# The first 512 features of each squared-ReLU layer computed as plain products, with the sums of activations made behind them

## The chip, the cores and the metric

The program runs on one NeuronCore of a Trainium2 chip. Five engines work side by side, each through its own instructions in its own order: TensorE (PE, with its weight loads shown apart as PEld), VectorE (DVE), ScalarE (ACT), GpSimd (POOL) and SyncE (SP), which here issues the transfers from device memory. An instruction waits on semaphores for what it needs from another engine, and whatever stands behind it on its engine waits too. The metric is the time of one execution on the device in microseconds (us); lower is better.

## The reference

The model is a stack of two layer pairs on 512 tokens of 1024 features: attention, a squared-ReLU layer, a gated recurrent block, a second squared-ReLU layer, and a last norm. The change touches the two squared-ReLU layers and the norm ahead of each:

```
def rmsnorm(x, g):
    y = xf * lax.rsqrt(jnp.mean(xf * xf, axis=-1, keepdims=True) + RMS_EPS)
    return (y * g.astype(jnp.float32)).astype(x.dtype)

def sq_relu_mlp(h, w1, w2):
    z = jax.nn.relu(jnp.einsum('bsd,df->bsf', h, w1))
    return jnp.einsum('bsf,fd->bsd', z * z, w2)
...
h = h + sq_relu_mlp(rmsnorm(h, norm_mlp[layer]), mlp_w1[layer], mlp_w2[layer])
```

Here w1 is 1024 x 4096 and w2 is 4096 x 1024, all in float32.

## The kernel before

Activations are held transposed: eight tiles hT[k] of 128 features by 512 tokens. To keep float32 accuracy on TensorE every operand is split into a high part (a cast to fp32r, by ACT) and a low part (the rest, by DVE), and `mm3` (L175) makes three matmuls of each product: high x high, high x low, low x high. So each weight unit (128 x 1024 numbers, 512 KB) costs a transfer (L104 or L110), an ACT cast into `wh` (L118) and a DVE subtraction into `wl` (L119). `plan` lists all units in the order in which TensorE wants them; `fetch` makes one, `want(n)` keeps `ahead` units made beyond the n that it hands out. Units live in the pool `wsp` (5 buffers); inside a squared-ReLU layer four more come from the pool `wx`, taken in turns of nine (L92). A unit's buffer is free when TensorE has read the unit that had it before. Raw weights go through three buffers `wr`.

A squared-ReLU layer (`mlp`, L530) handles the 4096 hidden features in eight groups g of 512. `up(g)` makes the group's first product by a seven-product scheme on 2 x 2 blocks (256 tokens or features to a block, Strassen's in Winograd's form): seven products named 1 to 7 of 24 matmuls of 128 x 256 each, in place of eight. It needs sums of weight blocks (units of kinds s1 to s4, five DVE additions of 128 x 1024 a group, L115 and L116) and sums of activation blocks t1 to t4. The latter are made once a layer: t1 where the norm's gain is applied (`split` with `blocks`, L203 to L207), and t2 to t4 by `sums_of` (L538), into tH and tL. `down(g, m)` makes the second product in plain form, 12 matmuls of 128 x 512 for each of eight tiles m of the output, and adds to hT[m]. Downs of group g-1 stand between the products of group g.

The norm's factor per token is taken late: the products run on activations that have only the gain, the squares are summed over features (`square`, L209, then `sums`, whose four little matmuls fill ss, then a square root on ACT and a reciprocal on DVE), and `rstd` (four more little matmuls, an ACT copy) spreads the factor `r` over partitions. It is used in `relu2` (L577). The work ahead of layer 0 is the last part of the attention's output projection (matmuls "wo", L333), ahead of layer 1 the recurrent block's ("ro", L812 and L814); after each tile of it `feed(m)` applies the gain.

The order on each engine is set by a scheduler ahead of time from the order of the calls and its own estimates; at run time it is fixed.

Of the kernel before, what the change touches and what calls it, by code (L numbers as in the profile page):

```python
# [15 lines left out]
P = 128  # L16
# [24 lines left out]
def trunk(ctx: ExitStack, tc: tile.TileContext, xT, cols, win, wqkv, wo, rwin, rga, rgx, rwo, w1, w2, out):  # L41
# [44 lines left out]
    def fetch():  # L86
# [65 lines left out]
    def add_mlp(layer):  # L152
        starts.append(len(plan))
        for g in range(9):
            if g < 8:
                rows, cs = (slice(0, T), slice(T, D)), (slice(g * T, g * T + U), slice(g * T + U, (g + 1) * T))
                srcs = [w1[layer][rows[k], cs[c]] for k, c in ((0, 0), (0, 1), (1, 1), (1, 0))]
                up_ = [(kind, 4, srcs) for kind in ("11", "s1", "12", "22", "s2", "s4", "s3")]
            else:
                up_ = []  # L160
            dn = [("plain", 4, [w2[layer][(g - 1) * T : g * T, u * U : (u + 1) * U]]) for u in range(4)] if g else []
            if up_ and dn:
                plan.extend(up_[0:2] + dn[0:1] + up_[2:3] + dn[1:2] + up_[3:5] + dn[2:3] + up_[5:7] + dn[3:4])
            else:
                plan.extend(up_ + dn)

# [5 lines left out]
    add_mlp(1)  # L172
    state["stop"] = starts[0]

# [16 lines left out]
    class Norm:  # L191
        def __init__(self, name, gain, c0=0, n=T, blocks=False):
            self.name, self.gain, self.acc, self.last, self.c, self.n = name, gain, None, None, slice(c0, c0 + n), n
            self.blocks, self.psum = blocks, mmp if blocks else atp

        def split(self, k):
            g = cst[:, self.gain + k : self.gain + k + 1]
            if not self.blocks or k >= KT // 2:
                S.activation(hnH[k], hT[k], AF.Copy, scale=g)
                V.scalar_tensor_tensor(hnL[k], hT[k], g, f(hnH[k]), ALU.mult, ALU.subtract)  # L200
# [21 lines left out]
        def feed(self, k):  # L222
            if k == 0:
                tc.keep_in_program_order(S.activation(spare, epsb, AF.Sqrt))
            self.split(k)
            if not self.blocks:
                self.square(k)


        def sums(self):  # L230
            nt = self.n // P
            ss = self.psum(f"{self.name}ss")
            parts = [self.acc] if self.last is None else [self.acc, self.last]
# [9 lines left out]
        def rstd(self):  # L243
            nt = self.n // P
            row = self.psum(f"{self.name}row")
            for t in range(nt):
# [8 lines left out]
    n0 = Norm("n0", C_MIX0)  # L255
    nm1 = Norm("nm1", C_MLP0, blocks=True)
    with ExitStack() as actx:
# [272 lines left out]
    def mlp(ly, norm, nxt, halves):  # L530
        with ExitStack() as mctx:
            pool = lambda name, bufs: mctx.enter_context(tc.tile_pool(name=f"{name}{ly}", bufs=bufs))
            sr, wx, tp, cp, zp = pool("sr", 1), pool("wx", 4), pool("t", 1), pool("c", 1), pool("z", 2)
            state.update(raw=sr, more=wx, units=0, ahead=7, stop=starts[ly + 1] if ly + 1 < len(starts) else None)
            prefetch(4)
            z, r, tH, tL = {}, [], [], []

            def sums_of(k):  # L538
                g, g2 = (cst[:, norm.gain + j : norm.gain + j + 1] for j in (k, k + 4))
                a = wk.tile([P, T], F32, name=f"ha{ly}{k}", tag="nsq", bufs=2)  # L540
                S.activation(a, hT[k], AF.Copy, scale=g)
                H = tp.tile([P, 3, U], F32R, name=f"tH{ly}{k}", tag=f"tH{k}")
                L = tp.tile([P, 3, U], F32R, name=f"tL{ly}{k}", tag=f"tL{k}")
                raw = cp.tile([P, 2, T], F32, name=f"ht{ly}{k}", tag="cB" if k % 2 else "cA")
                raw = raw.rearrange("p i (j c) -> p (i j) c", j=2)

                V.scalar_tensor_tensor(raw[:, 2], hT[k + 4][:, HI], g2, a[:, HI], ALU.mult, ALU.subtract)
                V.tensor_add(raw[:, 1], raw[:, 2], a[:, LO])
                V.scalar_tensor_tensor(raw[:, 0], hT[k + 4][:, LO], g2, raw[:, 1], ALU.mult, ALU.subtract)
                S.activation(H[:, 0:2], raw[:, 0:2], AF.Copy, scale=-1.0)  # L550
                V.scalar_tensor_tensor(L[:, 0:2], raw[:, 0:2], -1.0, f(H[:, 0:2]), ALU.mult, ALU.subtract)  # L551
                S.copy(H[:, 2], raw[:, 2])
                V.tensor_sub(L[:, 2], raw[:, 2], f(H[:, 2]))
# [10 lines left out]
            B11, t1, B21, B22 = own(0, LO), own(0, HI), own(4, LO), own(4, HI)  # L564
            t4, t2, t3 = (sum_(n) for n in range(3))

# [8 lines left out]

            def relu2(g, n, c, op, rr_):
                V.scalar_tensor_tensor(c, c, 0.0, rr_[:, None, :].to_broadcast([P, 2, T]), op, ALU.mult)  # L577
                S.activation(c, c, AF.Square)
# [4 lines left out]
                for i in range(2):  # L583
                    z[g, 2 * n + i] = (zH[:, i], zL[:, i])

            def up(g):

                acc = {}

                def one(n, xs):  # L590
                    acc[n] = (mmp if g == 0 and n in "54" else atp)(f"p{n}{ly}{g}")
                    product(acc[n], xs)
                    acc[n] = pair(acc[n])
# [19 lines left out]
                V.tensor_add(cA[:, :, HI], acc["3"], cA[:, :, HI])  # L613
                relu2(g, 0, cA, ALU.max, r[0])
                yield
# [3 lines left out]
                V.tensor_add(cB[:, :, HI], acc["5"], w)  # L619
                relu2(g, 1, cB, ALU.min, r[0])  # L620
                yield
# [59 lines left out]

    nm2 = Norm("nm2", C_MLP1, blocks=True)
    with ExitStack() as rctx:
# [172 lines left out]
```

## Time and profile before

| | us |
|---|---|
| median of three executions | 1104.23 (1103.11 to 1105.21) |
| the profiled execution | 1108.84 |
| its span, first to last instruction | 1107.1 |
| PE busy | 1080.5 (98%) |
| DVE busy | 875.9 (79%) |
| ACT busy | 538.5 (49%) |
| granted TensorE clock, mean | 0.989 |

A row of a timeline reads: start, duration, engine, line, operation, out<-in by the program's names, shape, count, and in brackets how long the engine stood idle before it and what ended that. A row of a view by windows gives for a stretch of time the busy microseconds of each engine with the number of instructions, the clock that TensorE was granted (1.00 is full), the share of the transfer engines' time and the rate. Matmul rows overlap, since they are pipelined: the step from one start to the next is what a matmul takes from TensorE, not its duration.

### The profile page before, as it was taken

How to read it: one execution, taken by the hardware profiler on the slowest of the kernel's cores; microseconds unless marked ns; L12 is line 12 of the kernel's file. 1: busy time of each engine (PE TensorE's matmuls, PEld its weight loads, DVE VectorE, ACT ScalarE, POOL GpSimd, SP SyncE). 2: the span in 40 equal slices, each digit the busy share in tenths (PEclk: the TensorE clock that was granted, in tenths of full speed). 3: DMA queues.
4: the chain of work that ended last, by engine and by line, in shares of the span. 5: the costliest groups of instructions: out<-in, count | busy, mean ns of one | idle time of the engine just before them, and what ended most of it. 6: DMA issues, size and time to landing. Idle time of an engine off the chain costs nothing.

```text
span 1107.1 us, 16096 instructions
## 1 busy us (share of the span) xinstructions
PE 1080.5 (98%) x6424; PEld 962.2 (87%) x6424; DVE 875.9 (79%) x1316; ACT 538.5 (49%) x794; POOL 11.0 (1%) x28
## 2 busy tenths in 40 slices
PE   9999999997999999999999999899999999999996
PEld 7889988887899899999988888789899999899996
DVE  7998888788886886777767689988897786777655
ACT  7766665465443443433435497456453343343321
POOL 1000000000000000000000000000000000000000
PEclk9999999998999999999999999999999999999998
DMA  8532441332334324313241122432433333323102
GB/s 266 136 101 72 115 118 55 109 100 77 100 92 152 96 62 138 105 58 115 59 151 58 58 76 77 123 124 82 129 107 103 116 95 94 106 82 99 57 1 77
DMA packets 113786, 109.10 MB, mean 99 GB/s; under 512 B 4016, under 2 KB 110640, under 8 KB 113712
## 3 DMA queue, kind: packets, MB, share of 16 engines
q1 hardware_dynamic: 113568, 108.02, 32.2%
q8 instruction: 50, 0.82, 0.3%
q14 instruction: 24, 0.20, 0.1%
q10 hardware_dynamic: 144, 0.07, 0.0%
HBM read 101.78 MB, written 2.10 MB: 94 GB/s over the span
## 4 chain that ended last, share of the span: by engine, by line
PE 82%; DVE 11%; DMA 3%; ACT 2%; issue 2%; SPq 0%; DVEq 0%; ACTq 0%
PE d L176 10%; PE d L177 10%; PE d L178 10%; PE p L176 9%; PE p L178 9%; PE p L177 9%; DVE wl L119 2%; PE x L384 1%; PE xb L176 1%; PE xb L178 1%; PE xb L177 1%; ACT wh L118 1%; DMA wr<-in_wqkv 1%; PE v L176 1%; PE oa L400 1%
## 5 line engine op out<-in xcount | busy, mean ns | idle before, releaser
L118 ACT CAST wh<-b 128x1024 fp32r<-128x1024 f32 x112 | 115.9, 1049 | 203.1 <-DVE b L116 76.8
L177 PE MATMUL d<-zL,wh 128*128 128x512 f32 (+1 forms) x544 | 205.9, 379 | 0.0
L176 PE MATMUL d<-zH,wh 128*128 128x512 f32 (+1 forms) x544 | 205.3, 380 | 0.0
L178 PE MATMUL d<-zH,wl 128*128 128x512 f32 (+1 forms) x544 | 204.7, 377 | 0.0
L119 DVE TENSOR_TENSOR wl<-b,wh 128x1024 fp32r<-128x1024 f32 x112 | 135.6, 1223 | 48.0 <-ACT wh L118 48.0
L118 ACT CAST wh<-wr 128x1024 fp32r<-128x1024 f32 (+1 forms) x121 | 125.7, 1041 | 94.7 <-PE p L177 45.6
L119 DVE TENSOR_TENSOR wl<-wr,wh 128x1024 fp32r<-128x1024 f32 (+1 forms) x121 | 146.8, 1213 | 21.7 <-ACT wh L118 21.5
L176 PE MATMUL p<-hnH,wh 128*128 128x256 f32 x512 | 147.2, 288 | 4.8 <-ACT wh L118 3.9
L178 PE MATMUL p<-hnH,wl 128*128 128x256 f32 x512 | 147.0, 287 | 2.1 <-DVE wl L119 2.1
L177 PE MATMUL p<-hnL,wh 128*128 128x256 f32 x512 | 147.3, 288 | 0.0
L178 PEld LDWEIGHTS d<-zH,wl 128*128 128x128 f32 x544 | 102.4, 188 | 19.2
L176 PEld LDWEIGHTS d<-zH,wh 128*128 128x128 f32 x544 | 102.5, 189 | 16.8 <-ACT zH L581 0.4
L631 DVE TENSOR_TENSOR hT<-d,hT 128x512 f32<-128x512 f32 x120 | 82.3, 688 | 43.9 <-PE d L178 43.7
L177 PEld LDWEIGHTS d<-zL,wh 128*128 128x128 f32 x544 | 102.7, 189 | 15.8
L178 PE MATMUL p<-tH,wl 128*128 128x256 f32 x384 | 108.9, 284 | 1.9 <-DVE wl L119 1.9
L176 PE MATMUL p<-tH,wh 128*128 128x256 f32 x384 | 109.2, 284 | 0.6 <-ACT tH L550 0.6
L177 PE MATMUL p<-tL,wh 128*128 128x256 f32 x384 | 108.8, 284 | 0.5 <-DVE tL L551 0.5
L176 PEld LDWEIGHTS p<-hnH,wh 128*128 128x128 f32 x512 | 100.3, 196 | 7.2 <-ACT wh L118 4.3
L178 PEld LDWEIGHTS p<-hnH,wl 128*128 128x128 f32 x512 | 100.2, 196 | 2.5 <-DVE wl L119 2.5
L177 PEld LDWEIGHTS p<-hnL,wh 128*128 128x128 f32 x512 | 100.4, 196 | 1.7
L176 PEld LDWEIGHTS p<-tH,wh 128*128 128x128 f32 x384 | 73.9, 193 | 2.5 <-ACT tH L550 0.8
L177 PEld LDWEIGHTS p<-tL,wh 128*128 128x128 f32 x384 | 73.7, 192 | 2.5 <-DVE tL L551 0.7
(331 smaller groups left out, 2065.8 us busy)
## 6 DMA issues: line engine op xcount, KB each, us to landing
wr<-in_w SPq DMA_DIRECT2D x64, 512.0 KB, 3.5
b<-in_w SPq DMA_DIRECT2D x64, 512.0 KB, 4.2
wr<-in_wqkv SPq DMA_DIRECT2D x20, 512.0 KB, 3.9
wr<-in_rwin SPq DMA_DIRECT2D x16, 512.0 KB, 3.5
wr<-in_wo SPq DMA_DIRECT2D x8, 512.0 KB, 3.5
wr<-in_rwo SPq DMA_DIRECT2D x8, 512.0 KB, 3.5
hT<-in_xT SPq DMA_DIRECT2D x8, 256.0 KB, 5.1
bias<-in_win SPq DMA_DIRECT2D x4, 512.0 KB, 4.5
```

The lines of the kernel that those rows point to most:

```text
L118: S.copy(H[:, :n], raw[:, :n])
L119: V.tensor_sub(L[:, :n], raw[:, :n], f(H[:, :n]))
L176: PE.matmul(acc, WH, XH, start=start, stop=False)
L177: PE.matmul(acc, WH, XL, start=False, stop=False)
L178: PE.matmul(acc, WL, XH, start=False, stop=stop)
L384: PE.transpose(b[:, c : c + P], pt[:, seg[t] + kt * P : seg[t] + (kt + 1) * P], ident)
L400: PE.matmul(oa[:, T - n :], vv, pH[:, c : c + n], start=False, stop=kt == 3)
L631: V.tensor_add(hT[m], acc, hT[m])
```

## The change

Five things change in each squared-ReLU layer.

1. Group 0 is made as plain products: four accumulators u0 to u3 of 128 features x 512 tokens, each over all eight activation tiles, from four plain weight units in place of seven. That is 96 matmuls of 128 x 512 in place of 168 of 128 x 256.
2. The gain is applied to whole tiles in `split`, so t1 is no longer made there. `sums_of` makes it as a fourth sum, and is called after the squares; the four calls stand ahead of the plain products in the code. Its raw tiles now lie in the buffers of zH and zL instead of those of cA and cB.
3. The norm's little matmuls come after u0 and u1 (`sums`) and after u2 (`rstd`).
4. `prefetch` no longer starts with the layer. The stop mark stands four units later, so the four plain units are fetched and cast under the projection that comes before.
5. `wx` has three buffers instead of four, `ahead` is 6 instead of 7, and the turn is eight instead of nine.

```
-            pool = state["more"] if state["units"] % 9 >= 5 else wsp
+            pool = state["more"] if state["units"] % 8 >= 5 else wsp
...
         for g in range(9):
+            if g == 0:
+                add(w1[layer], 0, 0, KT)
+                add(w1[layer], 0, U, KT)
+                continue
...
-    state["stop"] = starts[0]
+    state["stop"] = starts[0] + 4
...
         def split(self, k):
             g = cst[:, self.gain + k : self.gain + k + 1]
-            if not self.blocks or k >= KT // 2:
-                S.activation(hnH[k], hT[k], AF.Copy, scale=g)
-                V.scalar_tensor_tensor(hnL[k], hT[k], g, f(hnH[k]), ALU.mult, ALU.subtract)
-                return
-
-            d = wk.tile([P, T], F32, name=f"{self.name}d{k}", tag="nsq", bufs=2)[:, :U]
-            V.tensor_sub(d, hT[k][:, LO], hT[k][:, HI])
-            for src, c in ((hT[k][:, LO], LO), (d, HI)):
-                S.activation(hnH[k][:, c], src, AF.Copy, scale=g)
-                V.scalar_tensor_tensor(hnL[k][:, c], src, g, f(hnH[k][:, c]), ALU.mult, ALU.subtract)
+            S.activation(hnH[k], hT[k], AF.Copy, scale=g)
+            V.scalar_tensor_tensor(hnL[k], hT[k], g, f(hnH[k]), ALU.mult, ALU.subtract)
...
-            sr, wx, tp, cp, zp = pool("sr", 1), pool("wx", 4), pool("t", 1), pool("c", 1), pool("z", 2)
-            state.update(raw=sr, more=wx, units=0, ahead=7, stop=starts[ly + 1] if ly + 1 < len(starts) else None)
-            prefetch(4)
+            sr, wx, tp, cp, zp = pool("sr", 1), pool("wx", 3), pool("t", 1), pool("c", 1), pool("z", 2)
+            state.update(raw=sr, more=wx, units=0, ahead=6, stop=starts[ly + 1] + 4 if ly + 1 < len(starts) else None)
...
+                V.tensor_sub(raw[:, 3], a[:, LO], a[:, HI])
                 V.scalar_tensor_tensor(raw[:, 2], hT[k + 4][:, HI], g2, a[:, HI], ALU.mult, ALU.subtract)
                 V.tensor_add(raw[:, 1], raw[:, 2], a[:, LO])
                 V.scalar_tensor_tensor(raw[:, 0], hT[k + 4][:, LO], g2, raw[:, 1], ALU.mult, ALU.subtract)
+                S.copy(H[:, 2:4], raw[:, 2:4])
+                V.tensor_sub(L[:, 2:4], raw[:, 2:4], f(H[:, 2:4]))
...
-            for k in range(4):
-                sums_of(k)
-            for k in range(KT):
-                norm.square(k)
...
-            for n, _ in enumerate(up(0)):
-                if n == 1:
-                    norm.sums()
-                if n == 2:
-                    r.append(norm.rstd())
+            xs = [(hnH[k], hnL[k]) for k in range(KT)]
+            for k in range(KT):
+                norm.square(k)
+            for k in range(4):
+                sums_of(k)
+            cs = [cp.tile([P, 2, T], F32, name=f"c{n}{ly}0", tag=f"c{n}") for n in "AB"]
+            for n in range(2):
+                WH, WL = want(2)
+                accs = [mmp(f"u{ly}{2 * n + i}") for i in range(2)]
+                if n == 0:
+                    project(accs, PAIR, WH, WL, xs)
+                    norm.sums()
+                    first = accs
+                    continue
+                for i in range(2):
+                    project(accs[i : i + 1], PAIR[i : i + 1], WH, WL, xs)
+                    if i == 0:
+                        r.append(norm.rstd())
+                        for j in range(2):
+                            V.scalar_tensor_tensor(cs[0][:, j], first[j], 0.0, r[0], ALU.max, ALU.mult)
+                        square(0, 0, cs[0])
+                    V.scalar_tensor_tensor(cs[1][:, i], accs[i], 0.0, r[0], ALU.max, ALU.mult)
+                square(0, 1, cs[1])
```

Three places show how the order moves. Names end in the tile's number; unit 33 is the first of layer 0 in both kernels.

ACT, at the end of the attention, before (ax, pH and oH are the last heads' pieces; line 224 loads the table for the square root, ahead of the norm):

```order
L118 CAST wh32_2499<-wr32_2501 128x1024
L405 COPY ax13_2542<-oa13_2533 64x512
L388 CAST pH15_2562<-x015_2549 128x512
L388 CAST pH15_2562<-x115_2550 128x512
L410 CAST oH6_2545<-o6_2374 128x512
L388 CAST pH15_2562<-x215_2551 128x256
L405 COPY ax14_2580<-oa14_2570 64x512
L405 COPY ax15_2592<-oa15_2583 64x512
L410 CAST oH7_2595<-o7_2579 128x512
L224 ACT_TABLE_LOAD
L224 ACTIVATE spare_101<-epsb_100 128x1
```

The same stretch now:

```order
L118 CAST wh32_2499<-wr32_2501 128x1024
L118 CAST wh33_2599<-wr33_2601 128x1024
L220 ACT_TABLE_LOAD
L220 ACTIVATE spare_101<-epsb_100 128x1
L401 COPY ax13_2542<-oa13_2533 64x512
L384 CAST pH15_2562<-x015_2549 128x512
L384 CAST pH15_2562<-x115_2550 128x512
L406 CAST oH6_2545<-o6_2374 128x512
L384 CAST pH15_2562<-x215_2551 128x256
L401 COPY ax14_2580<-oa14_2570 64x512
L401 COPY ax15_2592<-oa15_2583 64x512
L406 CAST oH7_2595<-o7_2579 128x512
```

The cast of the first plain unit and the table load have moved ahead of the copies that finish the attention.

DVE, at the start of layer 0, before, the stretch that ends with the norm's reciprocal:

```order
L551 SCALAR_TENSOR_TENSOR tL03_2863<-ht03_2864,tH03_2862 128x512
L220 TENSOR_TENSOR nm1acc_2872<-nm1acc_2872,nm1sq3_2880 128x512
L116 TENSOR_TENSOR b12_33_2806<-b12_33_2806,b22_33_2804 128x1024
L220 TENSOR_TENSOR nm1acc_2872<-nm1acc_2872,nm1sq4_2883 128x512
L119 TENSOR_TENSOR wl42_2990<-wr42_2991,wh42_2989 128x1024
L220 TENSOR_TENSOR nm1acc_2872<-nm1acc_2872,nm1sq5_2886 128x512
L119 TENSOR_TENSOR wl38_2905<-b12_33_2806,wh38_2904 128x1024
L220 TENSOR_TENSOR nm1acc_2872<-nm1acc_2872,nm1sq6_2889 128x512
L119 TENSOR_TENSOR wl39_2910<-b11_33_2800,wh39_2909 128x1024
L220 TENSOR_TENSOR nm1acc_2872<-nm1acc_2872,nm1sq7_2892 128x512
L604 TENSOR_TENSOR cA00_2895<-p200_2988,w00_2897 128x2x256
L241 RECIPROCAL rt_102<-rt_102 128x4
```

The stretch around the reciprocal now:

```order
L549 SCALAR_TENSOR_TENSOR tL02_2858<-ht02_2859,tH02_2857 128x512
L544 TENSOR_TENSOR ht03_2872<-ht03_2872,ha03_2868 128x256
L547 TENSOR_TENSOR tL03_2871<-ht03_2872,tH03_2870 128x512
L545 SCALAR_TENSOR_TENSOR ht03_2872<-hT7_81,cst_73,ht03_2872 128x256
L116 TENSOR_TENSOR b21_37_2887<-b21_37_2887,b22_37_2889 128x1024
L549 SCALAR_TENSOR_TENSOR tL03_2871<-ht03_2872,tH03_2870 128x512
L237 RECIPROCAL rt_102<-rt_102 128x4
L116 TENSOR_TENSOR b22_37_2889<-b22_37_2889,b11_37_2885 128x1024
L119 TENSOR_TENSOR wl38_2896<-b21_37_2887,wh38_2895 128x1024
L119 TENSOR_TENSOR wl39_2902<-wr39_2903,wh39_2901 128x1024
L648 SCALAR_TENSOR_TENSOR cA00_2881<-u00_2911,nm1r_3009 128x512
L648 SCALAR_TENSOR_TENSOR cA00_2881<-u01_2912,nm1r_3009 128x512
```

All four sums of activations now stand between the squares and the reciprocal; unit 37 is the first block unit of group 1, 38 its second.

DVE, in layer 1, before, the stretch that makes the squared hidden features zL of group 0:

```order
L119 TENSOR_TENSOR wl158_7447<-b22_152_7239,wh158_7446 128x1024
L582 TENSOR_TENSOR zL100_7442<-cA10_7215,zH100_7441 128x1024
L618 TENSOR_TENSOR cB10_7216<-p410_7347,w10_7217 128x2x256
L619 TENSOR_TENSOR cB10_7216<-p510_7270,w10_7217 128x2x256
L119 TENSOR_TENSOR wl159_7489<-wr159_7490,wh159_7488 128x1024
L577 SCALAR_TENSOR_TENSOR cB10_7216<-cB10_7216,nm2r_7345 128x1024
L116 TENSOR_TENSOR b12_152_7241<-b12_152_7241,b22_152_7239 128x1024
L604 TENSOR_TENSOR cA11_7484<-p211_7581,w11_7486 128x2x256
L582 TENSOR_TENSOR zL101_7481<-cB10_7216,zH101_7480 128x1024
```

The same now:

```order
L119 TENSOR_TENSOR wl149_7118<-b12_146_7101,wh149_7117 128x1024
L119 TENSOR_TENSOR wl152_7264<-b22_146_7099,wh152_7263 128x1024
L571 TENSOR_TENSOR zL100_7225<-cA10_7091,zH100_7224 128x1024
L119 TENSOR_TENSOR wl150_7179<-wr150_7180,wh150_7178 128x1024
L650 SCALAR_TENSOR_TENSOR cB10_7092<-u13_7189,nm2r_7219 128x512
L119 TENSOR_TENSOR wl153_7295<-wr153_7296,wh153_7294 128x1024
L116 TENSOR_TENSOR b12_146_7101<-b12_146_7101,b22_146_7099 128x1024
L571 TENSOR_TENSOR zL101_7256<-cB10_7092,zH101_7255 128x1024
```

The second half of zL (zL101) hangs on the last plain product u13, and stands three rows behind its scaling.

On SP the four transfers of the plain units now come before the four of the next block units (b11, b21, b22, b12); on PE there are 144 fewer instructions in all.

More of the change, by code (lines that the diff above doesn't have):

```diff
@@ L160, in add_mlp @@
                 up_ = []
-            dn = [("plain", 4, [w2[layer][(g - 1) * T : g * T, u * U : (u + 1) * U]]) for u in range(4)] if g else []
-            if up_ and dn:
+            dn = [("plain", 4, [w2[layer][(g - 1) * T : g * T, u * U : (u + 1) * U]]) for u in range(4)]
+            if up_:
                 plan.extend(up_[0:2] + dn[0:1] + up_[2:3] + dn[1:2] + up_[3:5] + dn[2:3] + up_[5:7] + dn[3:4])
             else:
-                plan.extend(up_ + dn)
+                plan.extend(dn)
     add_mlp(0)
@@ L225, in feed @@
             self.split(k)
-            if not self.blocks:
+            if not self.late:
                 self.square(k)
@@ L244, in rstd @@
             nt = self.n // P
-            row = self.psum(f"{self.name}row")
+            row = atp(f"{self.name}row")
             for t in range(nt):
@@ L255, in trunk @@
     n0 = Norm("n0", C_MIX0)
-    nm1 = Norm("nm1", C_MLP0, blocks=True)
+    nm1 = Norm("nm1", C_MLP0, late=True)
     with ExitStack() as actx:
@@ L549, in sums_of @@
                 V.scalar_tensor_tensor(raw[:, 0], hT[k + 4][:, LO], g2, raw[:, 1], ALU.mult, ALU.subtract)
+                S.copy(H[:, 2:4], raw[:, 2:4])
+                V.tensor_sub(L[:, 2:4], raw[:, 2:4], f(H[:, 2:4]))
                 S.activation(H[:, 0:2], raw[:, 0:2], AF.Copy, scale=-1.0)
                 V.scalar_tensor_tensor(L[:, 0:2], raw[:, 0:2], -1.0, f(H[:, 0:2]), ALU.mult, ALU.subtract)
[L552 to L553 removed]
                 tH.append(H)
                 tL.append(L)
[L557 to L560 removed]
             own = lambda k0, c: [(hnH[k0 + k][:, c], hnL[k0 + k][:, c]) for k in range(4)]
             sum_ = lambda n: [(tH[k][:, n], tL[k][:, n]) for k in range(4)]
[L564 to L565 removed]
+            B11, B21, B22 = own(0, LO), own(4, LO), own(4, HI)
             def product(acc, xs):
@@ L574, in pair, with square @@
                 return acc.rearrange("p (j c) -> p j c", j=2)
-            def relu2(g, n, c, op, rr_):
-                V.scalar_tensor_tensor(c, c, 0.0, rr_[:, None, :].to_broadcast([P, 2, T]), op, ALU.mult)
+            def square(g, n, c):
                 S.activation(c, c, AF.Square)
@@ L584, in relu2 @@
                     z[g, 2 * n + i] = (zH[:, i], zL[:, i])
+            def relu2(g, n, c, op):
+                V.scalar_tensor_tensor(c, c, 0.0, r[0][:, None, :].to_broadcast([P, 2, T]), op, ALU.mult)
+                square(g, n, c)
             def up(g):
@@ L590, in one @@
                 def one(n, xs):
-                    acc[n] = (mmp if g == 0 and n in "54" else atp)(f"p{n}{ly}{g}")
+                    acc[n] = atp(f"p{n}{ly}{g}")
                     product(acc[n], xs)
@@ L633, in down @@
                     nxt(m)
-            for n, _ in enumerate(up(0)):
-                if n == 1:
-                    norm.sums()
-                if n == 2:
-                    r.append(norm.rstd())
+            xs = [(hnH[k], hnL[k]) for k in range(KT)]
[9 more added lines that the diff above has]
+                    project(accs, PAIR, WH, WL, xs)
+                    norm.sums()
+                    first = accs
[9 more added lines that the diff above has]
+                square(0, 1, cs[1])
+            t4, t2, t3, t1 = (sum_(n) for n in range(4))
             for g in range(1, 8):
@@ L679, in trunk @@
     mlp(0, nm1, n1.feed, False)
-    nm2 = Norm("nm2", C_MLP1, blocks=True)
+    nm2 = Norm("nm2", C_MLP1, late=True)
     with ExitStack() as rctx:
```

16 lines of the change are left out of this document (8 added, 8 removed).

## Prediction

> **What bounds the kernel now.** I read first the page's engine table, then windows over the two squared-ReLU layers, then what PE waited for in them. TensorE is the bound:
>
> ```profile
> PE 1080.5 (98%) x6424; PEld 962.2 (87%) x6424; DVE 875.9 (79%) x1316; ACT 538.5 (49%) x794; POOL 11.0 (1%) x28
> ```
>
> So a change gains only by less work on PE or by the 2% in which PE is idle or slowed. The next view says where those are: each layer's stretch cut at the first matmul of groups 0, 1, 2 (and 3 in layer 0).
>
> ```profile
> 249.70:282.80 33.10, 27.39 (x185) 26.38 (x184) 28.25 (x46) 18.41 (x28) 0.00 (x0) 0.85 0.24 72
> 282.80:328.40 45.60, 43.86 (x266) 39.65 (x265) 39.97 (x43) 20.28 (x21) 0.00 (x0) 0.96 0.37 110
> 328.40:370.40 42.00, 42.00 (x265) 38.15 (x264) 33.26 (x37) 16.26 (x17) 0.00 (x0) 1.00 0.32 101
> 751.60:773.60 22.00, 22.00 (x185) 21.94 (x184) 18.93 (x27) 13.84 (x19) 0.00 (x0) 1.00 0.32 96
> 773.60:820.10 46.50, 44.10 (x266) 39.80 (x265) 42.07 (x46) 20.39 (x21) 0.00 (x0) 0.96 0.37 114
> ```
>
> The reader is to see three things. Group 0 has the same 185 matmuls in both layers, and takes 33.10 us in layer 0 but 22.00 in layer 1, so 11.1 of the 33.1 are no matmul work. Group 1, 266 matmuls with the downs, takes 45.60 and 46.50 where an undisturbed group takes 42.00. And from group 2 on PE is busy without a gap. What PE waits for in layer 0's stretch (249 to 330) is weights and activation sums, 7.4 us in all:
>
> ```profile
> PE p L178 <- DVE wl L119: 3.7, 2, 1.9
> PE p L176 <- ACT wh L118: 1.7, 1, 1.7
> PE p L176 <- issue: 0.9, 1, 0.9
> PE p L176 <- ACT tH L550: 0.6, 1, 0.6
> PE p L177 <- DVE tL L551: 0.5, 1, 0.5
> ```
>
> While it waits DVE has no free moment (third figure below), and then TensorE runs at half its clock for 8 us (0.50):
>
> ```profile
> 260.00:264.00 4.00, 2.35 (x15) 1.95 (x16) 4.00 (x8) 2.37 (x5) 0.00 (x0) 1.00 0.00 0
> 264.00:268.00 4.00, 1.56 (x12) 1.17 (x10) 4.00 (x5) 3.46 (x5) 0.00 (x0) 0.92 0.45 133
> 268.00:272.00 4.00, 3.65 (x17) 3.65 (x18) 3.24 (x5) 0.58 (x1) 0.00 (x0) 0.50 0.84 249
> 272.00:276.00 4.00, 4.00 (x21) 4.00 (x21) 1.15 (x3) 1.20 (x2) 0.00 (x0) 0.50 0.43 142
> ```
>
> **The plain group on PE.** Rows of matmuls overlap, so I take steps from start to start. The last 24 wide matmuls ahead of layer 0 and the last 48 ahead of layer 1 begin and end with the first four rows; the last two frame the four little matmuls of `sums`, with their second pass.
>
> ```profile
> 244.11 0.40 PE L176 MATMUL wo<-oH,wh 128*128 128x512 f32 x1
> 249.48 0.39 PE L178 MATMUL wo<-oH,wl 128*128 128x512 f32 x1
> 740.61 0.39 PE L176 MATMUL ro<-gdH,wh 128*128 128x512 f32 x1
> 751.37 0.39 PE L178 MATMUL ro<-gdH,wl 128*128 128x512 f32 x1
> 763.36 1.05 PE L236 MATMUL nm2ss<-ones,nm2acc 128*128 128x2 f32 x8
> 764.28 0.36 PE L176 MATMUL p<-tH,wh 128*128 128x256 f32 x1
> ```
>
> (249.48 - 244.11) / 23 is 0.2335 us a matmul, (751.37 - 740.61) / 47 is 0.229. The little matmuls take 764.28 - 763.36 = 0.92; I take the same for the four of `rstd`, 1.8 for both. If nothing waits, group 0 is 96 x 0.2335 + 1.8 = 24.2 us in layer 0 and 96 x 0.229 + 1.8 = 23.8 in layer 1. Against the windows that is -8.9 and +1.8: in layer 1 the plain form by itself is a loss. With group 1 at the undisturbed 42.0, add -3.6 and -4.5. Sum with no wait: -15.2 us.
>
> **Does nothing wait?** More weighty than the work on DVE is its order, since all of it must fit under 24 us of PE. Steps of the kinds needed, again from start to start:
>
> ```profile
> 251.00 0.42 DVE L548 TENSOR_TENSOR ht<-ht,ha 128x256 f32<-128x256 f32 x1
> 251.33 0.43 DVE L553 TENSOR_TENSOR tL<-ht,tH 128x256 fp32r<-128x256 f32 x1
> 252.06 0.75 DVE L200 SCALAR_TENSOR_TENSOR hnL<-hT,cst,hnH 128x512 fp32r<-128x512 f32 x1
> 252.72 0.48 DVE L547 SCALAR_TENSOR_TENSOR ht<-hT,cst,ha 128x256 f32<-128x256 f32 x1
> 253.12 0.69 DVE L551 SCALAR_TENSOR_TENSOR tL<-ht,tH 128x512 fp32r<-128x512 f32 x1
> 253.72 0.42 DVE L548 TENSOR_TENSOR ht<-ht,ha 128x256 f32<-128x256 f32 x1
> 255.18 1.23 DVE L116 TENSOR_TENSOR b<-b,b 128x1024 f32<-128x1024 f32 x1
> 256.31 0.69 DVE L551 SCALAR_TENSOR_TENSOR tL<-ht,tH 128x512 fp32r<-128x512 f32 x1
> ```
>
> That is 0.33 for an addition of 256 columns, 0.40 for a scaled one, 0.60 for 512 columns, 0.66 for hnL, 1.13 for 1024 (I take 1.13 for `wl` and zL, which have the same size). A layer's DVE loses three `wl` and five block additions, 8 x 1.13 = 9.0, and in `split` 4 x (0.33 + 2 x 0.40 - 0.66) = 1.9; t1 in `sums_of` costs 4 x (0.33 + 0.60 - 0.33) = 2.4. One `sums_of` is now 2 x 0.33 + 2 x 0.40 + 2 x 0.60 = 2.7, four are 10.6.
>
> First edge, the reciprocal. Unit 37 takes unit 32's buffer (`wsp` has five), which the last wo matmuls read until 249.9, so its cast, 1.05 by the row of a cast below, ends at 251.0. From there DVE has wl37 1.13, hnL 0.66, the last square 0.60, the sums 10.6 and two block additions 2.3 ahead of the reciprocal: 266.3, with hand-offs to ACT some 266.7. PE comes to `rstd` after 72 wide matmuls, 0.92 and two more: 249.7 + 16.8 + 0.9 + 0.5 = 267.9. So 1.2 us to spare; in layer 1 the same sum gives 752.9 + 15.3 = 768.2 against 751.6 + 16.5 + 0.9 = 769.0, 0.8 to spare. I cost the sums at nothing: the plain products hide them. If that cover went they would cost up to 10.6 a layer.
>
> Second edge, zL. In layer 0 u03 ends at 273.9; one scaling 0.66 and four rows of 1.13 (zL000, wl41, wl43, zL001) end at 279.1. PE needs zL001 after p1 and p5 (48 narrow matmuls at 0.12, the step from 331.28 to 332.00, six rows on, in the last fence of this part: 5.8 us) and seven wide ones, at 281.3: free. In layer 1 the scaling of u13 stands behind zL100 and wl150, and these behind ACT's cast of unit 149, whose buffer is free at 772.5: cast, square, cast, 3 x 1.0, then zL100 1.13, wl150 1.13, scaling 0.7, square and cast 2.0, zL101 1.13, ends at 781.6; with full durations in place of steps 783.3. PE wants it at 782.7. A wait of 0 to 0.7: +0.5, nearer the full durations, since each of these rows waits for the one before it on the other engine.
>
> **The end of the attention.** The first plain unit is now cast ahead of the attention's last copies on ACT, and the table load with it:
>
> ```profile
> 216.50 1.05 ACT L118 CAST wh<-wr 128x1024 fp32r<-128x1024 f32 x1 [1.96 <-PE wo L177]
> 221.66 0.39 PE L177 MATMUL wo<-oL,wh 128*128 128x512 f32 x1
> 223.59 0.58 ACT L405 COPY ax<-oa 64x512 f32<-64x512 f32 x1 [6.04 <-PE oa L400]
> 224.93 1.29 DVE L389 TENSOR_TENSOR pL<-x,pH 128x512 fp32r<-128x512 f32 x2
> 225.68 0.50 PE L399 MATMUL oa<-pL,v 128*128 128x512 f32 x1
> 229.90 1.28 ACT L224 ACT_TABLE_LOAD   x1
> 231.20 0.20 ACT L224 ACTIVATE spare<-epsb 128x1 f32<-128x1 f32 x1
> ```
>
> Unit 33 takes unit 28's buffer, which the wo matmul of 221.66 reads until 222.05. So ACT casts at 222.1 (1.05), loads the table (1.28), does the small square root (0.1 as a step), and copies ax at 224.55 in place of 223.59. Queued behind it are the casts pH; pL follows them, and PE's oa of 225.68 came at once on the first half of pL (224.93 + 0.6). All move by 0.96, PE with them: +1.0. Its bounds are 0, if the wo matmuls that the new order puts between the oa fill the gap, and 2.4, if cast and load both fall on the path in full. [...]
>
> **One weight buffer less.** A group of 42.0 us uses 11 units, 3.8 us a unit. Matched in order of issue, every unit of groups 2 to 7 had its `wl` 16 to 31 us before its first matmul; the shortest is p5 of group 2:
>
> ```profile
> 313.46 1.23 DVE L119 TENSOR_TENSOR wl<-b,wh 128x1024 fp32r<-128x1024 f32 x1 [0.56 <-ACT wh L118]
> 331.28 0.28 PE L176 MATMUL p<-hnH,wh 128*128 128x256 f32 x1
> ...
> 332.00 0.28 PE L176 MATMUL p<-hnH,wh 128*128 128x256 f32 x1
> ```
>
> 331.28 - 314.7 is 16.6; minus 3.8 leaves 12.8, so I cost it at 0. Its bounds are 0 and rival (b). On SP the bytes are the same; the plain units' four transfers go ahead of the block units', which waited for the attention's memory anyway.
>
> **Sum.** -8.9 + 1.8 - 3.6 - 4.5 + 1.0 + 0.5 = -13.7 us. The profiled span 1107.1 becomes 1093.4, its execution of 1108.84 about 1095.1. That execution is 4.6 above the median of the runs, 1104.23, which becomes 1090.5.
>
> **Rivals.** (a) The chain on DVE and ACT comes later than I count, and PE waits again under the plain group. For it: DVE had 4.00 of 4.00 in the windows above, and my margins are 0.8 to 2.2 us. Against it: 8.5 us of DVE work a layer is gone. Price: half the 7.4 us of waits come back in each layer, so 13.7 - 7.4 = 6.3 gained: 1097.9.
>
> (b) Slower: the missing buffer shows. As a mechanism here: ACT stands in a cast that waits for PE to free a buffer while a square is queued behind it, so zL is late and PE waits once a group. It decides from 13.7 / 14 = 1.0 us in each of 14 groups; at 1.2 us it ends at 1107.3. The 12.8 us left speak against it. [...]
>
> (c) No change that can be told, within 0.2% (2.2 us, about what a measurement of this kernel tells from none): (a) in full, 2 x 7.4 given back, about 1105. That the change does not do what it says is out: PE has 144 instructions fewer.
>
> (d) Better than the sum: neither +1.0 nor +0.5 comes, 1089.0.
>
> **How the numbers follow.** My sum with its bounds, 1089 to 1092, and (d): 0.65. (a): 0.23. (b): 0.08. (c): 0.04. Hence faster 0.88, same 0.04, slower 0.08. The range goes below (d) by the 1 us by which the runs of one kernel differ, 1088.0, and up to most of (a), 1097.5; outside lie (b), (c) and the worst of (a), under 0.2.
>
> **What would show it.** Group 0 at 24.2 and 23.8 us, group 1 at 42 in both layers, no wait of PE on wl or tL there, the clock 1.00 at 268 to 276; a gap of about 1 us before oa near 225; group 2 on at 42.0 as before. It is wrong if PE waits for `rstd`, for zL, or once a group from group 2 on.

## The result and the profile after

The changed kernel takes 1093.43 us (median of four executions, 1092.29 to 1093.78) against 1104.72 (four, 1103.11 to 1105.52): a ratio of 0.9898, 95% interval 0.9881 to 0.9915, so 9.4 to 13.1 us faster, by the medians 11.3. The forecast was 1090.5 in a range of 1088.0 to 1097.5. The profiled execution took 1092.29 with a span of 1090.5.

The page's engine table of the changed kernel:

```profile
PE 1074.5 (99%) x6280; PEld 951.5 (87%) x6280; DVE 857.6 (79%) x1284; ACT 534.1 (49%) x778; POOL 10.5 (1%) x28
```

PE is busy for 6 us less and DVE for 18, but the span is 16.6 us shorter: most of what went was idle time of PE. The windows cut at the first matmuls of groups 0, 1 and 2 of each layer show where (duration, then for PE, PEld, DVE, ACT and POOL busy us and instructions, then the clock):

```profile
249.38:273.04 23.66, 23.66 (x114) 19.81 (x112) 23.27 (x40) 16.95 (x24) 0.00 (x0) 1.00 0.13 39
273.04:315.08 42.04, 42.04 (x266) 38.16 (x264) 34.10 (x37) 16.47 (x18) 0.00 (x0) 1.00 0.37 117
315.08:357.12 42.04, 42.04 (x266) 38.16 (x264) 31.67 (x34) 16.11 (x17) 0.00 (x0) 1.00 0.34 101
737.84:761.49 23.65, 23.65 (x113) 19.81 (x112) 23.11 (x39) 17.30 (x24) 0.00 (x0) 1.00 0.21 64
761.49:803.53 42.04, 42.04 (x265) 38.16 (x264) 33.92 (x37) 16.31 (x18) 0.00 (x0) 1.00 0.37 115
```

In every row PE is busy from end to end at full clock, though DVE is busy for 23.27 of 23.66 us in group 0. The list of what PE waited for no longer has any product of the two layers in it; it begins:

```profile
PE ro L180 <- ACT gdH L774: 1.6, 1, 1.6
PE ro L180 <- DVE y L769: 1.5, 1, 1.5
PE warm L413 <- POOL ones L76: 1.0, 1, 1.0
PE oa L395 <- DVE pL L385: 0.9, 1, 0.9
```

The two at the top stand in the recurrent block and were there before (1.7 and 1.6). The fourth is the price at the attention's end.

### The profile page after: what moved, and what is told of

Same layout as the page of the kernel before. It is cut to its first block, busy times and chain, and to the rows that moved or that the text cites. A ratio compares the mean times of both kernels' runs of the same rounds, so it can differ in the third digit from the quotient of the medians.

```text
span 1090.5 us, 15782 instructions
## 1 busy us (share of the span) xinstructions
PE 1074.5 (99%) x6280; PEld 951.5 (87%) x6280; DVE 857.6 (79%) x1284; ACT 534.1 (49%) x778; POOL 10.5 (1%) x28
## 4 chain that ended last, share of the span: by engine, by line
PE 87%; DVE 8%; ACT 2%; DMA 1%; issue 1%; DVEq 0%; SPq 0%; ACTq 0%
PE d L180 11%; PE d L181 11%; PE d L182 10%; PE p L182 9%; PE p L181 9%; PE p L180 9%; DVE wl L119 1%; PE u L180 1%; PE xb L180 1%; PE xb L182 1%; PE u L182 1%; PE u L181 1%; PE xb L181 1%; PE x L380 1%; PE wo L181 1%
## 5 line engine op out<-in xcount | busy, mean ns | idle before, releaser
L119 DVE TENSOR_TENSOR wl<-wr,wh 128x1024 fp32r<-128x1024 f32 (+1 forms) x129 | 156.6, 1214 | 26.5 <-ACT wh L118 22.5
L119 DVE TENSOR_TENSOR wl<-b,wh 128x1024 fp32r<-128x1024 f32 x98 | 118.7, 1222 | 35.3 <-ACT wh L118 35.2
L182 PE MATMUL p<-tH,wl 128*128 128x256 f32 x448 | 126.8, 283 | 0.0
L181 PE MATMUL p<-tL,wh 128*128 128x256 f32 x448 | 126.8, 283 | 0.0
L180 PE MATMUL p<-tH,wh 128*128 128x256 f32 x448 | 126.6, 282 | 0.0
L182 PE MATMUL p<-hnH,wl 128*128 128x256 f32 x336 | 95.1, 283 | 0.0
L181 PE MATMUL p<-hnL,wh 128*128 128x256 f32 x336 | 95.1, 283 | 0.0
L180 PE MATMUL p<-hnH,wh 128*128 128x256 f32 x336 | 94.9, 282 | 0.0
L182 PEld LDWEIGHTS p<-tH,wl 128*128 128x128 f32 x448 | 85.8, 192 | 0.0
L181 PEld LDWEIGHTS p<-hnL,wh 128*128 128x128 f32 x336 | 64.3, 191 | 1.6
L180 PEld LDWEIGHTS p<-hnH,wh 128*128 128x128 f32 x336 | 64.3, 191 | 1.6
```

The lines of the kernel that those rows point to most:

```text
L119: V.tensor_sub(L[:, :n], raw[:, :n], f(H[:, :n]))
L180: PE.matmul(acc, WH, XH, start=start, stop=False)
L181: PE.matmul(acc, WH, XL, start=False, stop=False)
L182: PE.matmul(acc, WL, XH, start=False, stop=stop)
```

## The experiments

Two theories stand against each other. Mine: group 0 was slow because the sums, the squares and the weights on DVE and ACT came too late, and the plain products give them a cover. The rivals: the gain belongs to something else in the change (a buffer, the order alone, the load alone), or to a lower clock that comes and goes by itself.

**The kernel before, once more.** No edit.

> The kernel before, profiled a second time. The profiled execution of before (1108.84 us) was 4.1 us above the median of its four runs, the one of the changed kernel 1.1 us below its median, so the two traces differ by 16.6 us and the medians by 11.3. Theory A (the surplus is a wait and clock drop that grew in that one execution, in the first group of layer 0): the new trace has a span near 1103, group 0 of layer 0 at about 28 to 29 us in place of 33.1, the stages from group 2 on as before. Theory B (the surplus lies in stages that the change does not touch, at the start or in the memory layer): group 0 of layer 0 is again 33.1 and group 1 45.6, and the missing 4 us are found elsewhere.

Measured: 1105.75 (ten executions, 1103.17 to 1108.36), ratio 1.0009 (0.9998 to 1.0020); the profiled one 1105.0, span 1103.2. Its windows for groups 0, 1, 2 of layer 0 and 0, 1 of layer 1:

```profile
249.30:279.40 30.10, 26.48 (x185) 25.40 (x184) 27.93 (x45) 18.44 (x28) 0.00 (x0) 0.83 0.25 78
279.40:325.20 45.80, 43.88 (x267) 39.66 (x266) 40.26 (x44) 20.29 (x21) 0.00 (x0) 0.96 0.35 111
325.20:367.20 42.00, 42.00 (x265) 38.15 (x264) 33.29 (x37) 16.28 (x17) 0.00 (x0) 1.00 0.33 101
748.20:770.30 22.10, 22.10 (x186) 22.00 (x185) 19.49 (x28) 13.85 (x19) 0.00 (x0) 1.00 0.31 96
770.30:816.30 46.00, 43.81 (x267) 39.68 (x266) 41.57 (x46) 20.41 (x21) 0.00 (x0) 0.96 0.37 115
```

Theory A holds: of the 3.9 us by which this span is shorter than the first one, 3.0 lie in group 0 of layer 0 (30.1 in place of 33.1, where I had expected 28 to 29). These windows also split the loss. The matmuls of group 0 take 22.0 us undisturbed (layer 1's first window). Here the group took 30.1: PE idle 30.1 - 26.5 = 3.6, busy too long 26.5 - 22.0 = 4.5. Most of the latter is the clock: its mean of 0.83 over these 30.1 us is a loss of 0.17 x 30.1 = 5.1 us, a part of which fell while PE was idle anyway. In the first profile the split was 5.7 and 5.4. So about half of the loss was not waiting but the half clock after it.

**Layer 0 alone.** Layer 1 as before, with its four extra buffers. The kernel holds both forms of the layer, `mlp` with the plain group and `mlp_s` as before; some lines of its edit of the kernel before:

```
+    PLAIN = (0,)
...
+            if g == 0 and layer in PLAIN:
...
-    mlp(1, nm2, None, True)
+    mlp_s(1, nm2, None, True)
```

> Only layer 0 takes the plain first group, the order of its sums, and the early fetch; layer 1 stays as before, four weight buffers included. By the two traces layer 0's groups 0 and 1 gained 13.0 us and the end of the attention lost 0.8. Theory A (4 us of the 13.0 were the surplus of one execution): 12.2 - 4.1 = about 8 us gained, near 1096.5. Theory B: all 12.2 gained, near 1092.5, faster than the full change.

Measured: 1094.41 (four), ratio 0.9910 (0.9896 to 0.9925): 8.3 to 11.5 us, by the medians 10.75, between the two theories. In the trace groups 0 and 1 of layer 0 are those of the full change, and those of layer 1 are as before:

```profile
249.96:273.62 23.66, 23.66 (x114) 19.81 (x112) 23.27 (x40) 16.93 (x24) 0.00 (x0) 1.00 0.13 37
273.62:315.66 42.04, 42.04 (x266) 38.16 (x264) 33.90 (x37) 16.43 (x18) 0.00 (x0) 1.00 0.38 118
738.33:760.37 22.04, 22.04 (x185) 21.98 (x184) 19.20 (x27) 13.84 (x19) 0.00 (x0) 1.00 0.31 97
760.37:806.57 46.20, 44.01 (x266) 39.70 (x265) 41.81 (x46) 20.39 (x21) 0.00 (x0) 0.96 0.37 115
```

**Layer 1 alone.** The same with `PLAIN = (1,)`, and `mlp_s` for layer 0.

> Only layer 1 takes the change, layer 0 stays as before. By the two traces its group 0 loses 1.6 us (22.0 to 23.65) and its group 1 gains 4.4 (46.5 to 42.0): about 2.8 us gained, near 1102. Rival: the waits of layer 1's group 1 come from what layer 0 or the fetch leaves and not from its own sums; then group 1 stays at 46.5 and the time rises by 1.6, near 1106.

Measured: 1102.64 (ten), ratio 0.9974 (0.9962 to 0.9986), 1.6 to 4.2 us faster, by the medians 2.5. Its two groups in layer 1:

```profile
749.30:773.00 23.70, 23.70 (x114) 19.82 (x113) 23.14 (x39) 17.30 (x24) 0.00 (x0) 1.00 0.21 65
773.00:815.00 42.00, 42.00 (x265) 38.14 (x264) 33.87 (x37) 16.24 (x17) 0.00 (x0) 1.00 0.37 115
```

As theory said: group 0 loses 1.6, group 1 gives back 4.0 to 4.5. The two layers add up: 10.75 + 2.5 = 13.3 against 11.3 for both, equal within the intervals. The gain is layer 0's for the most part.

**The missing buffer alone**, in the kernel before:

```
-            pool = state["more"] if state["units"] % 9 >= 5 else wsp
+            pool = state["more"] if state["units"] % 8 >= 5 else wsp
...
-            ..., pool("wx", 4), ...
-            state.update(..., ahead=7, ...)
+            ..., pool("wx", 3), ...
+            state.update(..., ahead=6, ...)
```

> The kernel before with three extra weight buffers in place of four, six units ahead in place of seven, nothing else. My theory: from group 2 on each unit has 12 us to spare, so these groups stay at 42.0; in groups 0 and 1 the units are late because of the vector engine and not of a buffer, so the time is the same within 1 us. Rival (the buffer matters): a wait per group of over 1.2 us, 14 groups, 17 us slower; or in groups 0 and 1 alone the waits for a weight grow by a unit's 3.8 us a layer, 1112.

Measured: 1102.19 (nine), ratio 0.9974 (0.9964 to 0.9984): 1.8 to 4.0 us faster. Neither theory had that: fewer buffers make this kernel faster. The profiled execution, at 1099.46, is the fastest of the nine, so its trace shows the kernel better than it mostly is. Group 0 of layer 0 is 28.0 us in it, group 1 of layer 1 is 44.2:

```profile
248.70:276.70 28.00, 23.89 (x185) 23.46 (x184) 24.73 (x42) 15.02 (x24) 0.00 (x0) 0.94 0.19 57
766.20:810.40 44.20, 42.60 (x266) 38.33 (x265) 42.45 (x46) 22.58 (x24) 0.00 (x0) 1.00 0.44 132
```

In group 0 PE idles 4.1 us, between the 5.7 and 3.6 of the two profiles of before, but it is busy too long by only 1.9 in place of 5.4 and 4.5. What moved on DVE in group 0 is, above all, the remainder `wl` of the first down's unit. In the first profile of the kernel before:

```profile
264.72 0.70 DVE L220 TENSOR_TENSOR nm1acc<-nm1acc,nm1sq 128x512 f32<-128x512 f32 x1
265.32 1.24 DVE L119 TENSOR_TENSOR wl<-wr,wh 128x1024 fp32r<-128x1024 f32 x1
266.46 0.70 DVE L220 TENSOR_TENSOR nm1acc<-nm1acc,nm1sq 128x512 f32<-128x512 f32 x1
```

It stands amid the late squares, 23 us ahead of its first use, because with four extra buffers in turn one is free for it that early. With three it comes behind them:

```profile
282.67 1.22 DVE L119 TENSOR_TENSOR wl<-wr,wh 128x1024 fp32r<-128x1024 f32 x1
```

That this one move makes the whole gain is not shown.

**Six ahead, but four buffers**, in the kernel before, to tell the two numbers apart:

```
-ahead=7
+ahead=6
```

> The kernel before with six units fetched ahead in place of seven and its four extra weight buffers kept. The kernel with three buffers and six ahead was 2.9 us faster. Theory A (the buffer itself did it: with a fourth one free, the unit of the first down projection is cast and its remainder made on VectorE in the midst of the late sums, some 20 us before it is needed): this kernel still has the buffer and that early remainder, 1104 to 1106. Theory B (the number ahead did it): 1101 to 1103.

Measured: 1104.18 (ten), ratio 0.9992 (0.9983 to 1.0002). Theory A, the buffer: the time is that of the kernel before, and the early remainder is still there:

```profile
264.30 1.21 DVE L119 TENSOR_TENSOR wl<-wr,wh 128x1024 fp32r<-128x1024 f32 x1
```

**Less load on DVE**, in the kernel before; the five block additions of weights of group 0 are left out in each layer:

```
-                if kind == name:
+                if kind == name and not any(i0 <= i < i0 + 7 for i0 in starts):
```

> The kernel before without the five block additions of weights of group 0 in each layer (5 x 1.13 us of VectorE a layer; the products of group 0 are then not those of the reference). Theory (VectorE's load makes the sums and the weight remainders late): the waits and the stretches at half clock of groups 0 and 1 shrink by about 5 us in each layer: 1094 to 1100. Rival (the waits come from the ScalarE casts, from buffers or from the transfers): within 1 us of 1105.

Measured: 1099.81 (five), ratio 0.9964 (0.9951 to 0.9977), 2.5 to 5.4 us faster: 11.3 us less work on DVE give 4.7, the low end of what theory expected. Group 1 is whole (42.1 and 42.0), but group 0 of layer 0 is no better than before, 31.2 us:

```profile
249.10:280.30 31.20, 25.99 (x186) 25.24 (x184) 29.33 (x46) 19.60 (x30) 0.00 (x0) 0.89 0.27 79
```

The rows of its longest wait on ACT and on PE:

```profile
266.90 0.62 ACT L219 ACTIVATE nm1sq<-hT 128x512 f32<-128x512 f32 x1
268.41 0.58 ACT L599 COPY w<-p 128x512 f32<-128x512 f32 x1 [0.89 <-DVE nm1acc L220]
...
269.05 0.39 PE L176 MATMUL p<-tH,wh 128*128 128x256 f32 x1 [3.89 <-ACT w L599]
```

The copy `w`, which empties the first product's accumulator, shares two buffers with the squares, and stands behind them on ACT; each square waits for DVE's addition of the one before. So it is not the load alone: the squares, put last, hold up what PE needs.

**The squares last**, in the changed kernel:

```
-            for k in range(KT):
-                norm.square(k)
             for k in range(4):
                 sums_of(k)
+            for k in range(KT):
+                norm.square(k)
```

> The changed kernel with the squares for the norm made after the four sums, as the kernel before made them, in place of ahead of them. Theory (the order on the vector engine matters more than its load, which is the same): the sum of squares is complete some 9 to 10 us later, PE stands at the norm's little matmuls near 261 and near 749: 8 to 12 us a layer, 1109 to 1118, so the new order is worth more than the whole gain. Rival (only the load counts): 1093 to 1096.

Measured: 1098.50 (four), ratio to the kernel before 0.9947 (0.9932 to 0.9962), 5.1 us more than the changed kernel. The order counts, but for a third of the least that I expected (1109, 16 us). The reason is in the rows of PE:

```profile
271.99 1.05 PE L232 MATMUL nm1ss<-ones,nm1acc 128*128 128x2 f32 x8 [0.22 <-DVE nm1acc L216]
274.35 1.16 PE L243 MATMUL nm1row<-ident,rt 128*128 128x128 f32 x8 [1.30 <-DVE rt L237]
```

The scheduler that orders the engines ahead of time put the norm's matmuls of layer 0 some 12 us later (271.99 in place of 260.3) and let plain products run in their place. What remains are waits of 0.2 and 1.3 us there, 0.3 and 1.3 in layer 1, and after layer 1's a clock of 0.50 (765 to 767 us).

**More load under the plain products**, in the changed kernel: one more subtraction of 1024 columns per sum.

```
+                pad = cp.tile([P, 2, T], F32, ..., tag="cB" if k % 2 else "cA")...
+                V.tensor_sub(pad, raw, raw)
```

> The changed kernel with one more subtraction of 1024 columns on the vector engine in each of the four sums (4 x 1.13 = 4.5 us a layer; its result is used by nothing). The order then also puts three weight remainders (3.4 us) ahead of the reciprocal in layer 0, so it comes 7.9 us later. The traces show the reciprocal 0.8 us ahead of the rstd matmuls in layer 0 and 0.6 ahead in layer 1. Theory (the plain products hide the sums, with under 1 us to spare): PE waits for the reciprocal, about 7 us in layer 0 and 4 to 7 in layer 1, and a stretch at half clock follows the gap as in the kernel before: 11 to 20 us slower than the changed kernel, 1104 to 1114. Rival (the cover is larger than the margins read from the trace, since group 0 as a whole has slack): 0 to 3 us slower, 1093 to 1097.

Measured: 1096.59 (four), ratio 0.9932 (0.9917 to 0.9947), 3.2 us more than the changed kernel: the rival's range. In layer 0:

```profile
249.40:275.20 25.80, 23.80 (x113) 19.60 (x112) 25.76 (x41) 13.78 (x20) 0.00 (x0) 1.00 0.11 31
...
274.30 1.16 PE L243 MATMUL nm1row<-ident,rt 128*128 128x128 f32 x8 [2.00 <-DVE rt L237]
```

The reciprocal comes at 274, 7.9 us later, as expected; but `rstd` moved behind the last plain product, so PE waits 2.0 us (1.6 in layer 1) and not 7.9 - 0.8 = 7.1. The room under the plain products is 5 us wider than the margin read from the trace: the 22 plain matmuls that stood behind `rstd` (22 x 0.229) now run ahead of it. DVE is full for the whole 25.8 us: here it is the bound.

**Work put into the waits**, in the kernel before, 42 more narrow matmuls in group 0 of layer 0:

```
                 def one(n, xs):
...
+                    if ly == 0 and g == 0 and n in "637":
+                        for _ in range(14):
+                            PE.matmul(acc[n][:, :U], hnH[0][:, :P], hnH[1][:, LO], start=True, stop=True)
                     product(acc[n], xs)
```

> The kernel before with 42 more narrow matmuls (0.12 us each, 5.0 us of PE work in all) in group 0 of layer 0, on operands that are long there, ahead of and among the products that wait; their result is overwritten. Theory (about half of what group 0 loses is not the waits of 5 to 7 us but the stretch at half clock that follows them): the matmuls lie in the waits, the clock stays at 1.00, and group 0 takes 26 to 28 us in place of 30 to 33: 1100 to 1103, faster with more work, with runs closer together than the 5.5 us of the kernel before. Rival (the clock has its own course, or the waits are what costs): the added work is paid in part or in full, 1105 to 1110.

Measured: 1103.24 (ten, 1102.27 to 1106.57), ratio 0.9988 (0.9979 to 0.9998): 5 us of work more, and at most 0.2% faster, not slower. In its trace group 0 takes 32.3 us:

```profile
249.00:281.30 32.30, 29.42 (x227) 28.66 (x226) 29.90 (x47) 18.47 (x29) 0.00 (x0) 0.95 0.27 82
```

Idle 2.9, matmuls 22.0 + 5.0, and busy too long by 29.4 - 27.0 = 2.4 in place of 4.5. A part of the loss was the clock, as theory said, but group 0 isn't faster; what this execution gained lies in the groups after it: 42.7 for group 1 of layer 0, but also 44.5 for group 1 of layer 1, which the edit does not touch. The runs spread over 4.3 us, no less than those of the kernel before beside them (1102.95 to 1105.90).

**The table load later**, in the changed kernel, behind the third hnH of layer 0:

```
-            if k == 0:
+            if k == (3 if self.name == "nm1" else 0):
                 tc.keep_in_program_order(S.activation(spare, epsb, AF.Sqrt))
```

> The changed kernel with the table load and its small square root moved behind the third hnH of layer 0; the early weight cast stays where it is. Theory: the wait of 0.92 us ahead of oa at the attention's end comes from cast and load together on ScalarE (1.05 + 1.28 between the release of the weight buffer and the copy of ax); without the load the cast ends at 222.0, before PE is done with the oa of 222.4, so the wait goes and the kernel gains 0.8 us: 1092.6. Rival: the order that follows there was late anyway, no gain, 1093.4.

> The version with the later table load again, beside the changed kernel. Theory: 0.7 us faster than it (by the trace, from the start of the second last block of oa to the layer's first matmul: 28.4 us in the changed kernel, 27.7 in this, 27.6 in the kernel before). Rival: no difference, both 1093.

> The changed kernel once more, on the same chip as the version with the later table load, for a comparison of the two: 1093.4 us, with runs within 1.5 us of each other.

Measured: 1092.10 (four); then, side by side on one chip, 1092.54 (1092.08 to 1092.60) against 1092.85 (1092.37 to 1093.12) for the changed kernel. The rows on ACT and PE in the changed kernel's trace:

```profile
220.94 1.05 ACT L118 CAST wh<-wr 128x1024 fp32r<-128x1024 f32 x1 [4.53 <-PE wo L181]
222.01 1.28 ACT L220 ACT_TABLE_LOAD   x1
...
223.53 0.58 ACT L401 COPY ax<-oa 64x512 f32<-64x512 f32 x1
...
225.62 0.50 PE L395 MATMUL oa<-pL,v 128*128 128x512 f32 x1 [0.92 <-DVE pL L385]
```

and with the later load, second trace:

```profile
222.45 0.59 ACT L401 COPY ax<-oa 64x512 f32<-64x512 f32 x1 [0.46 <-PE oa L396]
...
224.75 0.50 PE L395 MATMUL oa<-pL,v 128*128 128x512 f32 x1
```

The copy now waits for PE and not for ACT, and PE's wait is gone from the list. From the start of the block of oa two ahead of this one to the layer's first matmul the trace has 27.59 and 27.58 us in the two profiles of the kernel before, 28.41 and 28.33 in the two of the changed one, 27.72 and 27.70 with the later load. So the price was 0.8 us and 0.65 of it comes back; in the medians 0.3, too little to tell by them. It is the best version of the study, by the traces.

## Why the prediction was right, and where it was off

By its own terms, in us, against the two profiles of before:

| term | predicted | first profile to after | second profile to after |
|---|---|---|---|
| layer 0 group 0 | -8.9 | -9.4 | -6.4 |
| layer 1 group 0 | +1.8 | +1.6 | +1.6 |
| layer 0 group 1 | -3.6 | -3.6 | -3.8 |
| layer 1 group 1 | -4.5 | -4.5 | -4.0 |
| end of the attention | +1.0 | +0.8 | +0.8 |
| layer 1, zL101 | +0.5 | 0 | 0 |
| stages not touched | 0 | -1.5 | -0.9 |
| sum | -13.7 | -16.6 | -12.7 |

- **The sum against one execution.** This is the step that was off, by 3.0 us: "That execution is 4.6 above the median of the runs, 1104.23, which becomes 1090.5". It takes off the median what only that execution had lost: 3.0 of its surplus lay in group 0 of layer 0, the very stretch that the change removes. By the second profile, whose execution is within 1 us of the medians, the same working would give 13.7 - 3.0 + 0.2 - 0.5 = 10.4 gained where 11.3 were measured. That 13.7 came no further from it is in part luck: against the 12.7 between the spans of that profile and the one after, 2.3 us of small terms went the other way (stages not touched 0.9, the plain groups 0.7, zL101 0.5, the attention's end 0.2).
- **The range.** Its top of 1097.5 lies below 1097.9, the price of rival (a) itself, which had a chance of 0.23. Half of that with (b) and (c) is 0.24 outside, and not "under 0.2"; the result did not test it.
- **The plain group.** 24.2 and 23.8 predicted, 23.66 and 23.65 measured; the little matmuls take 0.8 a set and not 0.92, and the steps in layer 0 are those of layer 1.
- **Does nothing wait?** Right in both edges. The rows of layer 1, the tighter one:

```profile
754.24 0.18 DVE L237 RECIPROCAL rt<-rt 128x4 f32<-128x4 f32 x1
...
755.12 1.05 PE L243 MATMUL nm2row<-ident,rt 128*128 128x128 f32 x8
...
767.28 1.23 DVE L571 TENSOR_TENSOR zL<-cB,zH 128x1024 fp32r<-128x1024 f32 x1
```

  The reciprocal ends 16.6 us after the layer's start (predicted 16.6) and PE comes to it at 17.3 (17.4). zL101 ends 30.7 after the start, where I had PE want it at 31.1: the term of +0.5 did not come. The margins are real for this order, but they don't say what a later chain would cost: rival (a) was priced as if the order stayed, and the runs with padding and with late squares show that the scheduler moves PE's work into most of such a wait. Of the 7.4 us that this price rests on, 0.9 is "issue", for which the profile shows neither a weight nor a sum as the releaser.
- **The end of the attention.** Right in place and size: 0.92 of waiting against 0.96 predicted, 0.8 on the path. Its bound of 2.4, cast and load both on the path in full, was not reached. The row after the load begins 1.30 us after it (222.01 to 223.31), as in the kernel before (229.90 to 231.20), and no time passes ahead of it: the cast there ends at 220.94 + 1.05 = 221.99.
- **One weight buffer less.** Costed at 0 in the steady groups: right there, no wait from group 2 on and 42.04 a group. But I gave it no gain in groups 0 and 1, with "bounds 0 and rival (b)": a loss only. By itself it is worth -0.26% in the kernel before. How much of it is left inside the full change is open: four buffers in the changed kernel were not tried, since the fourth sum takes their room (8 tiles of 1 KB in each partition, as much as a `wh` and a `wl`).
- **The cause.** "Half the waits" of rival (a), the slower case (b) and no change (c) did not come. That DVE's load made group 0 slow is shown only in part: without the additions group 1 is whole and group 0 is not. The order of the squares, the fourth buffer with its early remainder, and the half clock after some of the gaps (group 0 of layer 0 had 0.85 and 0.83 in the mean) each had a share. What the traces do show is that the waits and the half clock of both groups are gone (PE busy for 23.66 of 23.66 and 42.04 of 42.04 us, at 1.00), and the two runs by layer that this is where the gain lies. Two parts of the change were not tried by themselves: the squares ahead of the sums while group 0 keeps its seven products, and the earlier fetch of its units. So it is not shown that group 0 had to be made as plain products.

## What to carry to other kernels

When a change removes waits, look at a second execution's trace before summing: a stretch with waits and clock drops varies from run to run (here 33.1 and 30.1 us for the same group), and the profiled run's surplus may be the thing that you take away. Split such a stretch into idle time and busy time beyond the undisturbed matmuls; here the second was 5.4 and 4.5 us, most of it the clock's at a mean of 0.85 and 0.83, and went with the gaps, to a clock of 1.00. A buffer more lets work be done earlier than needed, and on an engine that is late, early work for later can delay what is needed now: here a remainder of 1.24 us stood 23 us ahead of its first use, and with a buffer less and six units ahead the kernel was 1.8 to 4.0 us faster, though it is not shown that this remainder made the whole of it.

## What the runs showed of the hardware

The clock after a gap. The first row of each fence is a gap of PE in group 1 of layer 0, the rows below it are windows from the gap on. With three buffers:

```profile
281.40 0.38 PE L176 MATMUL p<-hnH,wh 128*128 128x256 f32 x1 [1.62 <-ACT wh L118]
280.00:282.00 2.00, 0.50 (x2) 0.30 (x2) 2.00 (x3) 2.00 (x3) 0.00 (x0) 1.00 0.00 0
282.00:284.00 2.00, 1.66 (x11) 1.53 (x12) 2.00 (x3) 2.00 (x3) 0.00 (x0) 1.00 0.08 14
284.00:286.00 2.00, 2.00 (x18) 1.97 (x17) 2.00 (x2) 1.28 (x3) 0.00 (x0) 1.00 0.93 262
```

In the kernel before, second profile:

```profile
284.37 0.58 PE L176 MATMUL p<-hnH,wh 128*128 128x256 f32 x1 [1.92 <-ACT wh L118]
282.00:284.00 2.00, 0.45 (x4) 0.24 (x3) 2.00 (x3) 2.00 (x3) 0.00 (x0) 1.00 0.01 4
284.00:286.00 2.00, 1.63 (x7) 1.63 (x8) 2.00 (x3) 2.00 (x3) 0.00 (x0) 0.60 0.00 0
286.00:288.00 2.00, 2.00 (x10) 1.81 (x9) 2.00 (x3) 1.15 (x2) 0.00 (x0) 0.55 0.41 112
```

The gap of 1.62 us was followed by a clock of 1.00, and so was the one of 2.00 us in the padded kernel (1.00 in the windows 274 to 276 and 276 to 278); the gap of 1.92 us was followed by 0.60 and 0.55. A gap of 2.18 us in group 1 of layer 1 was followed by 0.60 and 0.55 in the first profile of the kernel before (windows 779 to 781 and 781 to 783), where the group took 46.5 us. In the kernel with more matmuls that group has a gap of 2.2 us too and took 44.5, which is the undisturbed 42.0 and little more than the gap. So in these traces the length of the gap alone does not tell which clock follows; what else decides it is not shown.

The executions of the kernel before spread over 5.5 us (1102.41 to 1107.91 in 24), with mean clocks of 0.989 to 0.994, and those of the changed kernel, in whose trace PE has no gap in these groups, over 1.5 (1092.29 to 1093.78 in four), at 0.996 and 0.997. Four executions spread less than 24 by number alone, but on one chip four more of the changed kernel lay within 0.8 us and 19 of the kernel before within 3.0.
